# Branch A of a hybrid trunk layer: gate products between the projections, gates and scan handed out one piece per weight chunk

## The chip, the cores and the metric

The kernel runs on one core of a Trainium2 chip. The metric is the device time of one execution in microseconds. The median of three runs of the kernel before is 2580.13 us (2580.01 to 2581.76). The profile is one further execution of the same program.

## What is computed

One layer with 256 tokens, model width 4096 and two branches that read the same normalised input, then an output projection and a final norm. All inputs are float32.

```python
hn = rmsnorm(x, norm_g)
xa, ga, u, v, gb = split(hn @ w_in)                 # 5 x 4096 columns
xa = causal_depthwise_conv(xa, conv_w, conv_b)      # 4 taps
# branch A, 16 heads of 256 channels:
r = sigmoid(blockdiag(w_gate_a) xa + b_a)
i = sigmoid(blockdiag(w_gate_x) xa + b_x)
log_a = -8 * r * softplus(-lam)
h_t = exp(log_a_t) * h_(t-1) + sqrt(1 - exp(2 log_a_t)) * (i_t * xa_t)
ya = h * silu(ga)
# branch B, 16 head groups: yb = gelu(u) * (W_s layernorm(gelu(v)) + b) * silu(gb)
x = x + concat(ya, yb) @ w_out                      # 8192 x 4096
out = rmsnorm(x, final_g)
```

## The kernel before

Every float32 product is made of three float32r products: the operands are split into a high and a low part, and high times high, high times low and low times high are added in PSUM. The weights pass as one stream of chunks of 512 KB. For each chunk SyncE loads `raw` (four buffers), ScalarE rounds it into `hi`, VectorE subtracts to get `lo` (L64 to L66), and TensorE multiplies. `take` (L134) issues load and split of the chunk that is AHEAD = 3 further on; `hi` and `lo` have four buffers each, so the split of a chunk can begin when TensorE has left the chunk four before it. The order of chunks is the list `plan` (L69 to L86).

The elementwise work goes through a queue, `todo`: a finished product puts small functions there, and `work(n)` (L142), called after each chunk's products, takes n of them out and issues their instructions. `flush` issues all that is left. Within each engine, the framework's scheduler then sets the order of the built instructions by what it takes to be ready; the engines run their rows in that order.

Branch A (L533 to L566) takes two heads per round, in eight rounds. In a round TensorE runs four projections of 256 columns (`project`, L233; eight chunks of 16 products each), two for the heads' `xa` and two for their `ga`; then, after a `flush`, the gate products of both heads (`gate_products`, L473; 24 products a head, from one chunk of `w_g`); then the output projection of the round before (`out_project`, L286; 16 chunks of 12 products, and after every second chunk two additions `acc`, L284, on VectorE, which free two of the four PSUM buffers named `po`). `gate_values` (L487) reads the gate products on ScalarE: sigmoid twice, then tanh. A square root follows at L553; it needs another activation table than sigmoid and tanh, so an ACT_TABLE_LOAD stands ahead of it and another ahead of the next sigmoid. `queue_scan` (L499) has the rest of a head in seven steps: `one` for either channel half (add 1 and reciprocal on VectorE, L504 and L505), `two` and `three` (three products on GpSimd, L508, L509 and L513, and two instructions on VectorE), `four` (both scans, L518), `five` (GpSimd, L521) and `six` (the split of the result into `mix`). The steps of both heads are queued in pairs and handed out two per chunk in the output projection. The gate `ga` is collected at L271 to L273 (a copy on ScalarE, an addition on VectorE, a product on GpSimd) and made into a silu at L410 and L411.

In the last round the loads of `fg` (the final norm's gain, 2 MB on chip) and of eight further chunks of `w_out` that stay resident (`resident`, L530) go through the same SyncE queue. After it come eight chunks of the last products (L569) and sixteen slabs from the resident chunks (L579).

Of the kernel before, what the change touches and what calls it, by code (L numbers as in the profile page):

```python
# [7 lines left out]
F32 = mybir.dt.float32  # L8
# [18 lines left out]
def hybrid_trunk(ctx: ExitStack, tc: tile.TileContext, x, xt, par, w_p, w_t, w_g, ln_g, ln_b, ws_t, w_o, f_g, out):  # L27
    """Tokens are the moving or the stationary side of every product; a float32 product is three float32r
    passes over operands split exactly into 12 + 12 bits (high*high, high*low, low*high). The weights pass
    as one stream of chunks, split AHEAD chunks before their products; the elementwise work of a product is  # L30
    queued and handed out between the chunks that follow."""
# [23 lines left out]
    # a first use brings the activation tables in while the first loads run  # L55
# [27 lines left out]
    for e in range(8):  # L83
        plan += plan_p(X_A + 2 * e) + plan_p(X_A + 2 * e + 1) + plan_p(G_A + 2 * e) + plan_p(G_A + 2 * e + 1)
        plan += [("g", 2 * e, 0), ("g", 2 * e + 1, 0)] + plan_o(e - 1 if e else 15)
# [22 lines left out]
    def first_chunk(q):  # L108
        """The first chunks of x and of the weights, in step so that the products start early."""
# [24 lines left out]
    def take(*key):  # L134
        """The split chunk next in the plan; issues those up to AHEAD further on, and some queued work."""
        assert plan[issued[0] - len(ready)] == key, (plan[issued[0] - len(ready)], key)
        while issued[0] < len(plan) and len(ready) <= AHEAD:
            ready.append(load_chunk(plan[issued[0]]))
            issued[0] += 1
        return ready.pop(0)  # L140
# [5 lines left out]
    def flush():  # L146
        work(len(todo))

    def rsqrt_mean(dst, ssum, pool, n, name):
        """dst = 1 / sqrt(ssum / n + EPS), refined to float32."""  # L150
# [19 lines left out]
    # the tensor engine's clock rises under load: it is kept busy until the first chunks are there  # L170
# [27 lines left out]
    def queue_softplus():  # L198
        # 4 * softplus(-lambda): log1p(e^-|l|) = 2 atanh(z), z = s / (2 - s), s = sigmoid(-|l|)
# [33 lines left out]
    def project(block):  # L233
        """256 columns of the input projection, channels on partitions: [:, c, :256] + [:, c, 256:]."""
        ps = pj.tile([P, 2, 512], F32, tag="pj", name="ps")
        for q in range(KT // 4):
# [9 lines left out]
            work()  # L246
        return ps

    def project_t(slab):
        """512 columns of the input projection, tokens on partitions."""  # L250
# [17 lines left out]
    def collect(dst, ps, pool, tag):  # L268
        """dst = (the product in ps) * row scale."""
# [16 lines left out]
    def out_project(e, mix, extra=None):  # L286
        for n in range(8):
            ps = [po.tile([P, 512], F32, tag="po", name="po_t") for _ in range(2)]
            for q in range(2):
# [4 lines left out]
                work()  # L294
# [86 lines left out]
    def mix_tokens(i, ws, vn):  # L381
        """Position mixing of one head: chunk m of the tokens on partitions, [:, m, its 256 columns]."""
# [35 lines left out]
    for e in range(8):  # L418
# [16 lines left out]
        if pending is not None:  # L435
            out_project(*pending)
# [50 lines left out]
    def gate_values(h, both):  # L487
        gate = []
        for ps, bias, nm in zip(both, (B_A, B_X), "ri"):
            o = a2.tile([P, 2, S], F32, name=f"gate_{nm}")  # L490
            for c in range(2):
                nc.scalar.activation(o[:, c, :], ps[:, c, :], AF.Sigmoid, bias=prm_col(bias, 2 * h + c))
            gate.append(o)
        # t = tanh(-log a / 2): a = (1 - t) / (1 + t), sqrt(1 - a^2) = 2 sqrt(t) / (1 + t)
        for c in range(2):
            nc.scalar.activation(gate[0][:, c, :], gate[0][:, c, :], AF.Tanh, scale=sp4[:, 2 * h + c : 2 * h + c + 1])
        return gate

    def queue_scan(i, y, r, gi, g, mix):  # L499
        rec = a2.tile([P, 2, S], F32, name="rec")  # L500
        sq2 = a2.tile([P, 2, S], F32, name="sq2")
# [14 lines left out]
        def four():  # L516
            for c in range(2):
                nc.vector.tensor_tensor_scan(sq2[:, c, :], r[:, c, :], gi[:, c, :], 0.0, op0=ALU.mult, op1=ALU.add)  # L518
# [7 lines left out]
        return sq2, [lambda: one(0), lambda: one(1), two, three, four, five, six]  # L526
# [6 lines left out]
    for e in range(8):  # L533
        ys = []
# [6 lines left out]
        gs = []  # L541
        for i in range(2):
            g = a2.tile([P, 2, S], F32, name="ga")
            queue_silu(g, project(G_A + 2 * e + i), a3, "tmp")
            gs.append(g)
        flush()
        both = [gate_products(2 * e + i, *ys[i][1:]) for i in range(2)]
        mix = (mixp if e % 2 else mixa).tile([P, 4, 2, S], F32R, tag="mix", name="mix")
        gates = [gate_values(2 * e + i, both[i]) for i in range(2)]
        steps = []  # L550
        for i in range(2):
            sq2, st = queue_scan(i, ys[i][0], *gates[i], gs[i], mix)
            nc.scalar.activation(sq2, gates[i][0], AF.Sqrt, scale=4.0)  # L553
            steps.append(st)
        for pair in zip(*steps):
            todo.extend(pair)
# [7 lines left out]
        out_project(*pending, extra=None if e < 7 else lambda n: resident(n - 4) if n >= 4 else None)  # L564
        flush()
        pending = (e, mix)  # L566

# [87 lines left out]
```

## Time and profile before

| what | us |
|---|---|
| median of three runs | 2580.13 |
| span of the profiled execution | 2579.9 |
| TensorE busy in the span | 2542.5 (99%) |
| VectorE busy | 1599.4 (62%) |
| ScalarE busy | 1180.1 (46%) |
| GpSimd busy | 306.6 (12%) |

The profiled execution's own time, as far as the profile has it, is its span, 2579.9 us, which lies 0.2 us under the median of the runs. TensorE is the engine that sets the time; what matters of the others is where TensorE waits for them. Products overlap in TensorE's pipeline, so the starts of its rows are what tells its pace, and the profile's busy time does not show a slow restart as idle.

### The profile page before, as it was taken

Reading aid. Unit: us, or ns where it says so; the run is one execution under the profiler, and the core shown is the slowest. Engines: PE = TensorE matmul, PEld = TensorE weight load, DVE = VectorE, ACT = ScalarE, POOL = GpSimd, SP = SyncE. Lnnn points to the kernel's source line nnn. Section 1 sums busy time; section 2 is a strip of 40 time slices with the busy share of each in tenths; the row PEclk is TensorE's granted clock in tenths of the full one; section 3 lists DMA queues with packets and bytes.
Section 4 is the critical chain, followed back from the end, with each engine's and each line's share of the span. In section 5 each row is a group of like instructions: output and inputs, shape, how many; then the busy total and the mean of one; then the engine's idle time right before and its main releaser. Section 6 shows DMA issues by size and latency. Waiting matters only on the chain.

```text
span 2579.9 us, 32012 instructions
## 1 busy us (share of the span) xinstructions
PE 2542.5 (99%) x12306; PEld 2134.8 (83%) x12306; DVE 1599.4 (62%) x1731; ACT 1180.1 (46%) x1342; POOL 306.6 (12%) x234
## 2 busy tenths in 40 slices
PE   9999999999999999999999999999999999999997
PEld 7888888888888888888888888788888888788886
DVE  6544465564646565655555675858575766758586
ACT  7444444444444444444444534444453545344454
POOL 0000010110101010101000200202020201102034
PEclk9999999999999999999999999999999999999999
DMA  9655556565656565656555555555556565555564
GB/s 344 205 193 192 195 184 206 196 202 191 198 189 204 189 199 190 202 188 200 192 187 189 171 196 190 183 186 182 185 171 193 171 200 175 193 185 182 185 218 156
DMA packets 147849, 500.40 MB, mean 194 GB/s; under 512 B 16112, under 2 KB 26480, under 8 KB 147568
## 3 DMA queue, kind: packets, MB, share of 16 engines
q1 hardware_dynamic: 147552, 498.34, 58.8%
q8 instruction: 96, 1.57, 0.3%
q14 instruction: 57, 0.47, 0.1%
q10 hardware_dynamic: 144, 0.02, 0.0%
HBM read 494.10 MB, written 4.19 MB: 193 GB/s over the span
## 4 chain that ended last, share of the span: by engine, by line
PE 88%; DVE 8%; issue 3%; DMA 1%; ACT 1%; SPq 0%; DVEq 0%; ACTq 0%
PE ps L242 19%; PE ps L259 13%; PE ps L260 13%; PE ps L258 13%; PE ps L245 9%; PE po_t L278 6%; PE po_t L280 6%; PE po_t L279 6%; DVE lo L66 3%; DVE rec L504 1%; DVE sq L518 1%; DVE acc L284 1%; DVE rec L505 1%; DMA raw<-in_w_out 1%; ACT hi L65 1%
## 5 line engine op out<-in xcount | busy, mean ns | idle before, releaser
L66 DVE TENSOR_TENSOR lo<-raw,hi 128x1024 fp32r<-128x1024 f32 (+1 forms) x906 | 1135.8, 1257 | 893.2 <-ACT hi L65 892.7
L65 ACT CAST hi<-raw 128x1024 fp32r<-128x1024 f32 (+1 forms) x914 | 957.4, 1051 | 1281.1 <-PE ps L260 547.9
L242 PE MATMUL ps<-xs,hi 128*128 128x512 f32 x2048 | 722.3, 398 | 0.0
L259 PE MATMUL ps<-lo,xs 128*128 128x512 f32 x1536 | 598.0, 389 | 1.0 <-DVE lo L66 1.0
L258 PE MATMUL ps<-hi,xs 128*128 128x512 f32 x1536 | 598.8, 390 | 0.0
L260 PE MATMUL ps<-hi,xs 128*128 128x512 f32 x1536 | 597.6, 389 | 0.0
L245 PE MATMUL ps<-xs,lo 128*128 128x256 f32 x2048 | 574.9, 281 | 0.0
L242 PEld LDWEIGHTS ps<-xs,hi 128*128 128x128 f32 x2048 | 384.6, 188 | 94.4
L278 PE MATMUL po_t<-hi,mix 128*128 128x512 f32 x1026 | 400.6, 390 | 12.3 <-DVE acc L284 11.1
L279 PE MATMUL po_t<-lo,mix 128*128 128x512 f32 x1026 | 399.9, 390 | 10.3 <-DVE lo L66 10.3
L280 PE MATMUL po_t<-hi,mix 128*128 128x512 f32 x1026 | 399.2, 389 | 0.0
L245 PEld LDWEIGHTS ps<-xs,lo 128*128 128x128 f32 x2048 | 386.9, 189 | 0.3
L259 PEld LDWEIGHTS ps<-lo,xs 128*128 128x128 f32 x1536 | 288.6, 188 | 61.1 <-DVE lo L66 1.6
L258 PEld LDWEIGHTS ps<-hi,xs 128*128 128x128 f32 x1536 | 288.5, 188 | 60.3 <-ACT hi L65 0.7
L260 PEld LDWEIGHTS ps<-hi,xs 128*128 128x128 f32 x1536 | 288.5, 188 | 59.7
L278 PEld LDWEIGHTS po_t<-hi,mix 128*128 128x128 f32 x1026 | 192.6, 188 | 59.3 <-issue 15.7
L279 PEld LDWEIGHTS po_t<-lo,mix 128*128 128x128 f32 x1026 | 192.6, 188 | 52.7 <-DVE lo L66 13.7
L280 PEld LDWEIGHTS po_t<-hi,mix 128*128 128x128 f32 x1026 | 192.6, 188 | 39.9
L284 DVE TENSOR_TENSOR acc<-po_t,acc 128x512 f32<-128x512 f32 x256 | 164.4, 680 | 2.4 <-PE po_t L280 2.4
L340 POOL MEMSET ws<- 64x128 f32 x8 | 1.6, 201 | 723.2 <-DMA ws<-in_ws_t 386.5
L273 POOL TENSOR_TENSOR xp<-ev,rstd_bc 128x512 f32<-128x512 f32 x16 | 20.7, 1295 | 485.6 <-DVE ev L272 485.6
L358 POOL TENSOR_TENSOR v<-v,affine 128x256 f32<-128x256 f32 x32 | 38.7, 1227 | 286.1 <-DVE v L355 254.2
(124 smaller groups left out, 1073.3 us busy)
## 6 DMA issues: line engine op xcount, KB each, us to landing
raw<-in_w_t SPq DMA_DIRECT2D x382, 512.0 KB, 4.1
raw<-in_w_out SPq DMA_DIRECT2D x256, 512.0 KB, 3.3
raw<-in_w_p SPq DMA_DIRECT2D x256, 512.0 KB, 4.1
raw<-in_w_g SPq DMA_DIRECT2D x16, 512.0 KB, 3.3
acc<-in_x SPq DMA_DIRECT2D x8, 512.0 KB, 9.1
out<-acc SPq DMA_DIRECT2D x16, 256.0 KB, 2.8
xraw<-in_xt SPq DMA_DIRECT2D x14, 256.0 KB, 5.0
affine<-in_ln_g SPq DMA_DIRECT2D x16, 128.0 KB, 3.2
```

The source lines that it names most:

```text
L65: nc.scalar.copy(hi, src)
L66: sub.tensor_tensor(lo, src, hi.bitcast(F32), op=ALU.subtract)
L242: nc.tensor.matmul(ps[:, c, :], lhsT=hi[:, j, cs], rhs=xs[:, k, :, :].rearrange("p h t -> p (h t)"), start=k == 0, stop=False)
L245: nc.tensor.matmul(ps[:, c, 0:S], lhsT=lo[:, j, cs], rhs=xs[:, k, 0, :], start=False, stop=k == KT - 1)
L258: nc.tensor.matmul(ps[:, m, :], lhsT=xs[:, k, 0, ms], rhs=hi[:, j, :], start=k == 0, stop=False)
L259: nc.tensor.matmul(ps[:, m, :], lhsT=xs[:, k, 0, ms], rhs=lo[:, j, :], start=False, stop=False)
L260: nc.tensor.matmul(ps[:, m, :], lhsT=xs[:, k, 1, ms], rhs=hi[:, j, :], start=False, stop=k == KT - 1)
L278: nc.tensor.matmul(ps, lhsT=mix[:, k, 0, ms], rhs=hi[:, j, :], start=start, stop=False)
L279: nc.tensor.matmul(ps, lhsT=mix[:, k, 0, ms], rhs=lo[:, j, :], start=False, stop=False)
L280: nc.tensor.matmul(ps, lhsT=mix[:, k, 1, ms], rhs=hi[:, j, :], start=False, stop=stop)
L284: nc.vector.tensor_tensor(acc[:, m, ns], ps, acc[:, m, ns], op=ALU.add)
L358: nc.gpsimd.tensor_tensor(v[:, m, cs], v[:, m, cs], gain, op=ALU.mult)
```

## The change

In `plan` and in the round, the gate products of the first head move to between the second `xa` projection and the first `ga` projection, and those of the second head to between the two `ga` projections. The flush ahead of them is gone, except one in the last round, for the second gate's silu alone. `gate_values` becomes `queue_gates`: two sigmoids and then tanh with the square root are three queued pieces. `queue_scan` has eight pieces, with one scan each for the two channel halves. `project` and branch A's `out_project` hand out one piece per chunk; branch B and the last round keep two. The pieces of the first head's scan are queued when the second head's gate products have been issued.

```diff
-        plan += plan_p(X_A + 2 * e) + plan_p(X_A + 2 * e + 1) + plan_p(G_A + 2 * e) + plan_p(G_A + 2 * e + 1)
-        plan += [("g", 2 * e, 0), ("g", 2 * e + 1, 0)] + plan_o(e - 1 if e else 15)
+        plan += plan_p(X_A + 2 * e) + plan_p(X_A + 2 * e + 1) + [("g", 2 * e, 0)] + plan_p(G_A + 2 * e)
+        plan += [("g", 2 * e + 1, 0)] + plan_p(G_A + 2 * e + 1) + plan_o(e - 1 if e else 15)
...
-            work()
+            work(1)
         return ps
...
-    def out_project(e, mix, extra=None):
+    def out_project(e, mix, extra=None, items=1):
...
-                work()
+                work(items)
...
-    def gate_values(h, both):
+    def queue_gates(h, both):
+        r, gi = (a2.tile([P, 2, S], F32, name=f"gate_{nm}") for nm in "ri")
+        sq2 = a2.tile([P, 2, S], F32, name="sq2")
+        def sigmoid(o, ps, bias):
...
+        def decay():
+            for c in range(2):
+                nc.scalar.activation(r[:, c, :], r[:, c, :], AF.Tanh, scale=sp4[:, 2 * h + c : 2 * h + c + 1])
+            nc.scalar.activation(sq2, r, AF.Sqrt, scale=4.0)
+        todo.append(lambda: sigmoid(r, both[0], B_A))
+        todo.append(lambda: sigmoid(gi, both[1], B_X))
+        todo.append(decay)
+        return r, gi, sq2
...
-        return sq2, [lambda: one(0), lambda: one(1), two, three, four, five, six]
+        todo.extend([lambda: one(0), lambda: one(1), two, three, lambda: four(0), lambda: four(1), five, six])
...
-        gs = []
         for i in range(2):
+            gates = queue_gates(2 * e + i, gate_products(2 * e + i, *ys[i][1:]))
+            if i:
+                queue_scan(*scans.pop())
             g = a2.tile([P, 2, S], F32, name="ga")
-            queue_silu(g, project(G_A + 2 * e + i), a3, "tmp")
-            gs.append(g)
-        flush()
-        both = [gate_products(2 * e + i, *ys[i][1:]) for i in range(2)]
...
+            ps = project(G_A + 2 * e + i)
+            scans.append((i, ys[i][0], *gates, g, mix))
+            if e == 7 and i:
+                rest, todo[:] = todo[:], []
+                queue_silu(g, ps, a3, "tmp")
+                flush()
+                todo.extend(rest)
+            else:
+                queue_silu(g, ps, a3, "tmp")
+        queue_scan(*scans.pop())
```

VectorE, first round of branch A, the kernel before: from the copy of the second `ga` product (`ev`) on, that is from the gate products to the third pair of output chunks. `lo` is a chunk's split, `acc` the additions that free PSUM.

```order
L272 TENSOR_TENSOR ev<-ps,ev 128x512
L504 TENSOR_SCALAR rec<-gate_r 128x256
L505 RECIPROCAL rec<-rec 128x256
L66 TENSOR_TENSOR lo<-raw,hi 128x1024
L504 TENSOR_SCALAR rec<-gate_r 128x256
L505 RECIPROCAL rec<-rec 128x256
L504 TENSOR_SCALAR rec<-gate_r 128x256 x2
L505 RECIPROCAL rec<-rec 128x256 x2
L66 TENSOR_TENSOR lo<-raw,hi 128x1024 x2
L284 TENSOR_TENSOR acc<-po_t,acc 128x512 x2
```

Both heads' four reciprocals stand here in one run of rows, ahead of two splits and the first additions; this run leaves the place.

The same engine with the change, in the second `ga` projection: from the copy of the first `ga` product on. The splits named here are those of this projection's chunks 3 to 7 and of the first output chunks; `mix` is the first head's.

```order
L272 TENSOR_TENSOR ev<-ps,ev 128x512
L66 TENSOR_TENSOR lo<-raw,hi 128x1024 x2
L511 TENSOR_SCALAR rec<-gate_r 128x256
L66 TENSOR_TENSOR mix<-ga,mix 128x2x256
L512 RECIPROCAL rec<-rec 128x256
L511 TENSOR_SCALAR rec<-gate_r 128x256
L512 RECIPROCAL rec<-rec 128x256
L66 TENSOR_TENSOR lo<-raw,hi 128x1024 x2
L517 TENSOR_SCALAR gate_r<-gate_r 128x512
L66 TENSOR_TENSOR lo<-raw,hi 128x1024
L521 TENSOR_TENSOR gate_r<-gate_r,rec 128x512
```

The second head's reciprocals have come into the projection, behind the split of the first head's `mix` and ahead of the splits of chunks 5 and 6; the first head's have gone into the projection before it.

SyncE, last round, the kernel before: the loads from the two gate chunks (`in_w_g`) to the end; `in_w_out` are output chunks, the resident ones among them.

```order
L98 DMA raw<-in_w_g 128x1024 x2
L98 DMA raw<-in_w_out 128x1024 x6
L563 DMA fg<-in_f_g 128x4096
L98 DMA raw<-in_w_out 128x1024 x26
L610 DMA out<-acc 128x512 x16
```

The load of `fg` stands behind the sixth output chunk here. With the change, from that round's second gate chunk on (`in_w_p` are chunks of the projections):

```order
L98 DMA raw<-in_w_g 128x1024
L98 DMA raw<-in_w_p 128x1024 x8
L98 DMA raw<-in_w_out 128x1024 x9
L571 DMA fg<-in_f_g 128x4096
L98 DMA raw<-in_w_out 128x1024 x23
```

The load of `fg` has moved three output chunks back in the queue, and the gate chunk ahead of a projection.

## Rows read from the trace of the kernel before

**Rows 1.** Page, part 1: busy us of each engine (share), instructions.
```profile
PE 2542.5 (99%) x12306; PEld 2134.8 (83%) x12306; DVE 1599.4 (62%) x1731; ACT 1180.1 (46%) x1342; POOL 306.6 (12%) x234
```

**Rows 2.** Stretches: from:to length, busy by engine, PEclk, DMA share, GB/s.
```profile
1376.30:2519.00 1142.70, 1123.16 (x6019) 959.80 (x6017) 778.45 (x848) 528.62 (x612) 183.48 (x131) 1.00 0.57 186
...
1376.30:1465.13 88.83, 88.83 (x515) 78.33 (x513) 49.61 (x56) 37.43 (x40) 5.77 (x8) 1.00 0.58 190
...
1470.89:1518.20 47.31, 44.86 (x197) 36.24 (x196) 43.76 (x49) 22.56 (x29) 14.65 (x9) 1.00 0.54 178
```

**Rows 3.** Who TensorE waited for in branch A: us, times, longest.
```profile
PE po_t L279 <- DVE lo L66: 10.3, 8, 1.3
PE po_t L278 <- DVE acc L284: 8.2, 8, 1.0
```

**Rows 4.** Timeline of TensorE, first output projection: start, us, what, idle before.
```profile
1479.07 0.39 PE L278 MATMUL po_t<-hi,mix 128*128 128x512 f32 x1
1480.76 0.50 PE L279 MATMUL po_t<-lo,mix 128*128 128x512 f32 x1 [1.30 <-DVE lo L66]
1481.09 0.40 PE L280 MATMUL po_t<-hi,mix 128*128 128x512 f32 x1
...
1483.15 0.39 PE L280 MATMUL po_t<-hi,mix 128*128 128x512 f32 x1
1483.66 0.47 PE L278 MATMUL po_t<-hi,mix 128*128 128x512 f32 x1
...
1494.44 0.39 PE L280 MATMUL po_t<-hi,mix 128*128 128x512 f32 x1
1495.85 0.47 PE L278 MATMUL po_t<-hi,mix 128*128 128x512 f32 x1 [1.02 <-DVE acc L284]
```

**Rows 5.** Timeline of VectorE in the same stretch.
```profile
1471.12 1.38 DVE L504 TENSOR_SCALAR rec<-gate_r 128x256 f32<-128x256 f32 x1
...
1476.27 3.35 DVE L505 RECIPROCAL rec<-rec 128x256 f32<-128x256 f32 x2
1479.55 3.37 DVE L66 TENSOR_TENSOR lo<-raw,hi 128x1024 fp32r<-128x1024 f32 x2
...
1490.51 3.48 DVE L518 TENSOR_TENSOR_SCAN sq<-gate_r,gate_i 128x256 f32<-128x256 f32 x4
```

**Rows 6.** Timelines of ScalarE and GpSimd in the same stretch.
```profile
1469.55 0.63 ACT L410 ACTIVATE sg<-ga 128x512 f32<-128x512 f32 x1 [0.20 <-POOL ga L273]
...
1473.18 1.28 ACT L553 ACT_TABLE_LOAD   x1
1474.47 1.15 ACT L553 ACTIVATE sq<-gate_r 128x512 f32<-128x512 f32 x2
...
1493.47 0.62 ACT L65 CAST mix<-ga 128x512 fp32r<-128x512 f32 x1 [2.82 <-POOL ga L521]
...
1468.20 1.31 POOL L273 TENSOR_TENSOR ga<-ev,rstd_bc 128x512 f32<-128x512 f32 x1 [18.62 <-DVE ev L272]
1470.25 2.10 POOL L411 TENSOR_TENSOR ga<-ga,sg 128x512 f32<-128x512 f32 x1 [0.74 <-ACT sg L410]
...
1491.85 1.59 POOL L521 TENSOR_TENSOR ga<-ga,sq 128x512 f32<-128x512 f32 x1 [7.79 <-DVE sq L518]
```

**Rows 7.** One line and one group: durations (ns min/median/max); busy us, mean ns, idle before.
```profile
L504 DVE TENSOR_SCALAR rec<-gate_r x32: 284/1113/1393, 1468.0 to 2476.3; 128x256 f32<-128x256 f32 x32
...
L66 DVE TENSOR_TENSOR lo<-raw,hi 128x1024 fp32r<-128x1024 f32 (+1 forms) x906 | 1135.8, 1257 | 893.2 <-ACT hi L65 892.7
```

**Rows 8.** The second round's four projections as one stretch.
```profile
1517.73:1608.17 90.44, 90.44 (x513) 78.38 (x512) 49.41 (x55) 38.13 (x39) 5.41 (x6) 1.00 0.57 186
```

**Rows 9.** The end: chain of waits; TensorE's waits after 2519 us; DMA issue, KB, us to landing.
```profile
2498.84 3.46 DMA raw<-in_w_out
...
PE po_t L278 <- DVE acc L284: 2.9, 3, 2.0
...
fg<-in_f_g SPq DMA_DIRECT2D x1, 2048.0 KB, 7.5
```

More of the change, by code (lines that the diff above doesn't have):

```diff
@@ L435, in hybrid_trunk @@
         if pending is not None:
-            out_project(*pending)
+            out_project(*pending, items=2)
         mix = mixp.tile([P, 4, 2, S], F32R, tag="mix", name="mix")
@@ L485, in gate_products, with queue_scan @@
         return both
-    def gate_values(h, both):
-        gate = []
-        for ps, bias, nm in zip(both, (B_A, B_X), "ri"):
-            o = a2.tile([P, 2, S], F32, name=f"gate_{nm}")
+    def queue_gates(h, both):
+        r, gi = (a2.tile([P, 2, S], F32, name=f"gate_{nm}") for nm in "ri")
+        sq2 = a2.tile([P, 2, S], F32, name="sq2")
+        def sigmoid(o, ps, bias):
             for c in range(2):
                 nc.scalar.activation(o[:, c, :], ps[:, c, :], AF.Sigmoid, bias=prm_col(bias, 2 * h + c))
[L493 to L499, printed above, removed]
+        def decay():
[6 more added lines that the diff above has]
+        return r, gi, sq2
+    def queue_scan(i, y, r, gi, sq2, g, mix):
         rec = a2.tile([P, 2, S], F32, name="rec")
-        sq2 = a2.tile([P, 2, S], F32, name="sq2")
         def one(c):
@@ L514, in three, with four @@
             nc.vector.tensor_tensor(r, r, rec, op=ALU.mult)
-        def four():
-            for c in range(2):
-                nc.vector.tensor_tensor_scan(sq2[:, c, :], r[:, c, :], gi[:, c, :], 0.0, op0=ALU.mult, op1=ALU.add)
+        def four(c):
+            nc.vector.tensor_tensor_scan(sq2[:, c, :], r[:, c, :], gi[:, c, :], 0.0, op0=ALU.mult, op1=ALU.add)
         def five():
@@ L533, in hybrid_trunk @@
     for e in range(8):
+        mix = (mixp if e % 2 else mixa).tile([P, 4, 2, S], F32R, tag="mix", name="mix")
         ys = []
@@ L540, in hybrid_trunk @@
             ys.append((y, yh, yl))
-        gs = []
+        scans = []
         for i in range(2):
+            gates = queue_gates(2 * e + i, gate_products(2 * e + i, *ys[i][1:]))
+            if i:
+                queue_scan(*scans.pop())
             g = a2.tile([P, 2, S], F32, name="ga")
-            queue_silu(g, project(G_A + 2 * e + i), a3, "tmp")
-            gs.append(g)
-        flush()
-        both = [gate_products(2 * e + i, *ys[i][1:]) for i in range(2)]
[L548 to L556, printed above, removed]
+            ps = project(G_A + 2 * e + i)
[8 more added lines that the diff above has]
+        queue_scan(*scans.pop())
         if e == 7:
@@ L563, in hybrid_trunk @@
             nc.sync.dma_start(fg, f_g.partition_broadcast(P))
-        out_project(*pending, extra=None if e < 7 else lambda n: resident(n - 4) if n >= 4 else None)
-        flush()
+        out_project(*pending, extra=None if e < 7 else lambda n: resident(n - 4) if n >= 4 else None, items=1 if e < 7 else 2)
         pending = (e, mix)
+    flush()
     for n in range(8):
```

## The prediction, made before the changed kernel was run

> **What bounds the kernel now.** I began with the page's busy times: TensorE works 99% of the span and no other engine more than 62% [rows 1]. So a change gains only where TensorE stands still, and costs only where it makes TensorE wait. The stretches tell how much there is: in branch A's eight rounds TensorE is busy 1123.16 of 1142.70 us [rows 2], so 19.5 us are idle. The waits name the places: in each of the eight rounds one wait for a split `lo` (10.3 us in all) and one for an addition `acc` (8.2) [rows 3]; 18.5 of the 19.5 us. The reader is to see that the count is eight, one of each per round, and that all lie in the output projection: the four projections and the gate products have none (88.83 busy of 88.83 in the first round's projections [rows 2]).
>
> The idle column is not all that such a wait costs, so I went to TensorE's timeline and took starts [rows 4]. From 1481.09 to 1483.15 nine steps take 2.06 us, 0.23 each. The product at 1480.76 starts 1.69 us after the one before it, 1.46 too late; the next follows after 0.33 instead of 0.23, 0.10 more for a slow restart; at 1483.66 0.51 have passed, 0.28 too many; at 1495.85 1.41, 1.18 too many; behind each of the last two I count another 0.08 of restart, by the 0.10 above. Together 3.18 us a round, **25.4 us in eight rounds**. This is the pool that the change can empty.
>
> Why VectorE is late is in its own timeline [rows 5]. After the gate products the reciprocals of both heads run together; one pair takes 3.35 us, and only behind it come two splits (3.37). The split that TensorE waits for at 1480.76 is the first of them. Later four scans in one run take 3.48 us, and the addition that frees PSUM at 1495.85 is behind them. A chunk of the output projection lasts 12 x 0.23 = 2.7 us, and VectorE was busy 43.76 of 47.31 us in that stretch [rows 2]: it is nearly full there, and a run of 3.4 us is not absorbed. In the projections it was busy 49.61 of 88.83 us [rows 2]; there is the room.
>
> **The change part by part.** TensorE's instructions are the same in number and kind; the gate chunks only stand elsewhere in the stream. Nothing is saved on any engine. VectorE's four reciprocals, the two `rec` additions and the scans move from the output projection into the two `ga` projections, one head in each. By the built order VectorE's output-projection rows keep only splits, additions, one copy addition and one `mix` split. From 43.76 us I take four reciprocals (2 x 3.35 = 6.7), the scans (3.48) and one split of `mix` (half of what they were), and it falls to about 33 of 44 us: both waits of [rows 3] should go. **Term 1: -25.4 us**, if nothing new comes.
>
> What is new: the second `ga` projection carries the second head's gates and the first head's silu, product and `mix`. Its order on VectorE: splits of chunks 3 and 4, one `rec` addition, the split of `mix`, reciprocal, `rec` addition, reciprocal, split of chunk 5. VectorE waits for `mix` there, with the splits of chunks 5, 6 and 7 queued behind the wait, and TensorE waiting for those. I count from the start of chunk 0 of that projection. In the trace the product with `rstd` on GpSimd began at 1468.20, 3.1 us after its projection ended at 1465.13 [rows 2, 6]; the second gate products (24 x 0.12 = 2.9 us, half of the 5.76 from 1465.13 to 1470.89, [rows 2]) now lie between, so it begins at +0.2. From its start to the end of the silu product took 4.15 us (1468.20 to 1470.25 + 2.10), then the product with the scan 1.59 and ScalarE's rounding of `mix` 0.62 [rows 6]: `mix` is there at +6.6. Then VectorE: two `rec` additions, two reciprocals 3.35, the `mix` split 0.68 (half a chunk's 1.26 and a little over, from [rows 7]), the split of chunk 5 1.26. With the additions at their least, 0.28 each, that is 5.85 us, ready at +12.4. With both at their worst, 1.39 each [rows 7], and the split of chunk 5 delayed by one GpSimd product of 1.31 [rows 6], it is +15.9. TensorE needs it at 5 x 90.44/32 = +14.1 [rows 8]. So the cover is 1.7 us at best and short by 1.8 at worst. I take a value near the good end, because one of the two additions waits for nothing on GpSimd: its next product there needs the very reciprocal that follows. One blocked addition gives +13.5, 0.6 to spare. Chunks 6 and 7 follow with less behind them. **Term 2: +1.2 us**, 0.15 a round; bounds 0 and 8 x 2.0 = 16 us.
>
> The long row of 1.38 against 0.28 for the same addition is VectorE standing while GpSimd runs: the row at 1471.12 ends with GpSimd's product, 1470.25 + 2.10 [rows 5, 6]. The Trainium skill ("SBUF — State Buffer", section "Who interferes with whom") states that the two engines share one port pair, that whoever starts first holds it for its whole instruction and the other blocks fully, and that a VectorE instruction with two SBUF inputs is among those that block. By that rule this change does harm: it puts six GpSimd products beside the splits of one projection. The trace agrees; with the rule in force at every step the sum is the bad bound of term 2, without it the good one.
>
> ScalarE loads its activation table four times a round instead of twice: 16 more of 1.28 us [rows 6], 20.5 us on an engine that was busy 37.43 of 88.83 us in the projections [rows 2]. Two of them lie in the second `ga` projection and the next rounding is not due before VectorE gets to it, so I count zero; that cover is the 5.85 us of VectorE work above, and without it a load costs its 1.28 a round.
>
> The gate chunks' loads are single ones among projection chunks now. No load row is added; SyncE's queue passes them in the same order as TensorE uses them. Count zero.
>
> The pace of TensorE in the projections is the open size. The first round's four took 88.83 us, the second's 90.44 [rows 2, 8], for the same products, with no wait in either: 1.61 us more. The first round is entered from the end of branch B, the others straight from output products. Now the two `ga` projections of a round are entered from gate products, which no row shows. Bounds: all seven later rounds gain half of 1.61 (-5.6 us); or the first round loses its half (+0.8). I take 0, since gate products pass into a projection without a break, as the output products do in those later rounds. **Term 3: 0**, bounds -5.6 and +0.8.
>
> The end: after 2519 us TensorE waits three times for additions, 2.9 us, with restarts some 3.3 [rows 4, 9]. The chain there goes through loads of `w_out` from 2498.84 on [rows 9], which waited for `raw` buffers that late splits (behind scans and `mix`) held. With those splits in time the loads start earlier. Against it, the 2 MB of `fg` (7.5 us to landing [rows 9]) stand three chunks later, closer to the resident loads. Bounds: all 3.3 gained, or 3 lost. **Term 4: -2.2 us**, two thirds, since `fg` lands before the eight resident loads begin.
>
> Sum: 2579.9 - 25.4 + 1.2 + 0 - 2.2 = 2553.5 for the profiled execution; the median lies 0.2 above its span: **2553.7 us**.
>
> **The rivals.** (a) VectorE late in the second `ga` projection: the bad bound above, 0.5 to 1.8 us a round with restart, 4 to 16 us: 2556.5 to 2568. For it: VectorE and GpSimd do collide in rows. Against: collisions at every step are needed. (b) The pace: the `ga` projections run at the first round's pace, 2548. (c) The end keeps or adds to its waits: 2556 to 2559. (d) Table loads delay ScalarE. The sum has a load at 1.28 us, and in the trace the square root starts 0.01 us after the load ends [rows 6]. If each load cost twice that, the silu's sigmoid and the tanh would come 1.28 later, which eats the 0.6 to spare and leaves it 0.7 short, with a restart 0.8 a round: 6.4 us instead of term 2's 1.2, 2559. The Trainium skill ("ScalarE: Activation LUTs", section "What ACT_TABLE_LOAD costs") states a drain of about 1.38 us behind each load, and its rules ask to do all of one set before switching, which this change breaks; the trace does not show that drain. (e) The waits only move: each round's 3.2 us come back as waits for splits in the `ga` projections. No change, 2580; it needs the bad bound of term 2 and 1.4 us more in each round. (f) **Slower**: the wait for `mix` on VectorE. Should the first head's scan slip out of its own projection by a chunk (2.8 us), and the GpSimd products ahead of `mix` that ran at 1.31 and 1.59 take 2.1 as the third did, `mix` comes at +6.6 + 2.8 + 1.3 = +10.7 and the split of chunk 5 at +16.5 to +20.0, 2.4 to 5.9 us late. With a restart each that is 20 to 48 us lost in eight rounds against the 27.4 (terms 1 and 4) gained: up to 2600. It decides from 3.4 us late on.
>
> **How the numbers follow.** My forecast (all or nearly all waits gone, 2551 to 2556) 0.50; (a) 0.20; (b) 0.13; (c) 0.06; (d) 0.04; (e) 0.04; (f) 0.03. The range runs from (b), with the end's 3.3 gained too, to most of (a): 2546 to 2565. A measurement of this kernel tells 0.2%, 5 us, from no change: faster is all but (e) and (f), 0.93; same 0.04; slower 0.03.
>
> **What would show it.** Right: no wait of `po_t` for `lo` or `acc` in rounds 1 to 7, and a round of 143.0 us, gate product to gate product (1465.13 to 1608.17 [rows 2, 8]), down to about 139.9. Term 2 shows as a wait of `ps` (L245's product) for `lo` in the second `ga` projection. Term 3 shows in the length of eight chunks behind a gate product: 22.2 or 22.6 us. Term 4 shows in the three waits after the last round. Wrong: waits of over 0.6 us a round for `lo` in the `ga` projections, or a VectorE row of `mix` that starts later than 7 us into the second of them.

## The result, and the profile after

The changed kernel takes 2552.38 us (median of four runs, 2550.41 to 2553.06) against 2580.07 before; the ratio is 0.989, with a 95% interval of 0.9876 to 0.9904. It is faster by 1.1%, and 2553.7 had been predicted. The profiled execution took 2552.63 us for a span of 2550.8, so 1.8 us lie outside the span. The page of the kernel after, part 1, against [rows 1]:

```profile
PE 2530.9 (99%) x12306; PEld 2137.6 (84%) x12306; DVE 1625.9 (64%) x1731; ACT 1203.3 (47%) x1360; POOL 322.0 (13%) x234
```

TensorE has the same 12306 products. VectorE is busy 26.5 us longer with the same 1731 instructions. The largest part are the sixteen rows of L517 (L510 before), which take 1.52 instead of 0.42 us each, 17.6 us in all; in the second round such a row runs from 1601.97 on, beside a GpSimd product that lasts from 1601.04 to 1603.20. ScalarE has 18 more instructions and 23.2 us more, which is 18 table loads of 1.28. All TensorE's waits of the kernel after, against [rows 3] (line and tile that waited, for whom; us, times, longest):

```profile
PE po_t L278 <- DVE acc L284: 3.7, 1, 3.7
PE warm L173 <- POOL ones L169: 1.1, 1, 1.1
PE ps L259 <- DVE lo L66: 0.9, 2, 0.7
```

Of the sixteen waits in the eight rounds none is left. The two last lines belong to the kernel's start; the first is new and lies at the end, behind the product of 2488.62. Stretches of the second round of the kernel after (length, busy by engine, PEclk, DMA share, GB/s): its two `xa` projections, its two `ga` projections, its output projection, and last all of the round.

```profile
1513.74:1536.34 22.60, 22.60 (x130) 19.61 (x128) 10.79 (x10) 8.40 (x8) 0.00 (x0) 1.00 0.59 190
1536.34:1558.95 22.61, 22.61 (x131) 19.62 (x129) 13.84 (x18) 9.50 (x10) 1.40 (x2) 1.00 0.58 187
1561.83:1584.02 22.19, 22.19 (x131) 19.56 (x129) 21.99 (x26) 11.88 (x14) 7.32 (x5) 1.00 0.48 157
1586.90:1609.09 22.19, 22.19 (x130) 19.56 (x129) 19.16 (x18) 13.55 (x19) 10.72 (x6) 1.00 0.49 162
1609.09:1652.65 43.56, 43.56 (x194) 36.04 (x193) 30.73 (x34) 19.64 (x20) 4.75 (x3) 1.00 0.67 214
...
1513.74:1652.65 138.91, 138.91 (x753) 120.15 (x752) 99.94 (x107) 68.54 (x78) 24.19 (x16) 1.00 0.59 190
```

The reader is to see three things. VectorE's load has moved: 30.73 of 43.56 us in the output projection, 21.99 and 19.16 of 22.19 in the `ga` projections; these are now the fullest places. The two projections behind gate products take 22.19 us, the two behind other products 22.60. And the clock is at its upper level throughout (1.00, 2.4 GHz). The last round with all that follows it, to the end of the span, of before and of after (each from a window of its own):

```profile
2376.05:2579.90 203.85, 185.56 (x951) 156.01 (x949) 138.10 (x170) 94.98 (x131) 57.97 (x34) 0.98 0.56 186
```

```profile
2347.22:2550.80 203.58, 185.60 (x951) 158.25 (x949) 145.75 (x170) 98.55 (x134) 59.30 (x34) 0.96 0.56 187
```

So the gain by stages, from TensorE's starts:

| stage | before | after | difference | predicted |
|---|---|---|---|---|
| to the first round | 1376.30 | 1375.57 | -0.7 | 0 |
| first round | 141.43 | 138.17 | -3.3 | -3.0 |
| next six rounds | 858.32 | 833.48 | -24.8 | -18.2 |
| last round and end | 203.85 | 203.58 | -0.3 | -5.2 |
| span | 2579.9 | 2550.8 | -29.1 | -26.4 |

The rounds gained more than was predicted and the end gained nothing. The end, in TensorE's timeline of the kernel after (start, us, what, idle before):

```profile
2488.62 0.39 PE L280 MATMUL po_t<-hi,mix 128*128 128x512 f32 x1
2492.74 0.76 PE L278 MATMUL po_t<-hi,mix 128*128 128x512 f32 x1 [3.73 <-DVE acc L284]
2493.30 0.63 PE L279 MATMUL po_t<-lo,mix 128*128 128x512 f32 x1
```

and the granted clock there, in stretches:

```profile
2492.70:2498.50 5.80, 5.76 (x14) 4.54 (x15) 5.80 (x5) 1.54 (x3) 2.38 (x1) 0.51 0.62 200
2498.50:2510.00 11.50, 11.50 (x52) 9.51 (x51) 10.81 (x14) 6.05 (x6) 6.17 (x3) 1.00 0.64 208
```

One stall of 4.12 us from start to start, 3.89 too many. Behind it the granted clock is 0.51, the lower level of 1.2 GHz, for 5.8 us: fourteen products, nearly all 0.43 instead of 0.23 us from start to start, 2.7 us more. Together 6.6 us are lost there, against 3.8 in the kernel before (7.0 from 2440 on by the same count, less the 3.2 of its last round). Behind TensorE's last product the rest of the span is 1.4 us longer too (14.5 against 13.1): VectorE's scaling of the first token half, in a row of 1.77 us beside GpSimd's products, stands ahead of the last additions. In the kernel before such a row (1.78 us, from 2563.67 on) came ahead of the last products, and TensorE waited 0.2 us there. VectorE's timeline of the kernel after, where the last product starts at 2536.27:

```profile
2535.67 1.77 DVE L613 SCALAR_TENSOR_TENSOR acc<-acc,rs,fg 128x512 f32<-128x512 f32 x1
2537.36 0.68 DVE L599 TENSOR_TENSOR acc<-po_t,acc 128x512 f32<-128x512 f32 x1
2537.96 0.74 DVE L613 SCALAR_TENSOR_TENSOR acc<-acc,rs,fg 128x512 f32<-128x512 f32 x1
2538.62 1.34 DVE L599 TENSOR_TENSOR acc<-po_t,acc 128x512 f32<-128x512 f32 x3
```

### The profile page after: what moved, and what is told of

It is laid out like the page before. It is cut to its first block, busy times and chain, and to the rows that moved or that the text cites. A ratio compares the mean times of both kernels' runs of the same rounds, so it can differ in the third digit from the quotient of the medians.

```text
span 2550.8 us, 32030 instructions
## 1 busy us (share of the span) xinstructions
PE 2530.9 (99%) x12306; PEld 2137.6 (84%) x12306; DVE 1625.9 (64%) x1731; ACT 1203.3 (47%) x1360; POOL 322.0 (13%) x234
## 4 chain that ended last, share of the span: by engine, by line
PE 97%; DMA 1%; DVE 1%; ACT 0%; POOL 0%; issue 0%; SPq 0%; DVEq 0%; ACTq 0%
PE ps L242 19%; PE ps L259 14%; PE ps L260 14%; PE ps L258 14%; PE ps L245 10%; PE po_t L278 8%; PE po_t L280 8%; PE po_t L279 8%; DMA raw<-in_w_out 1%; PE pgate L482 1%; PE pgate L483 1%; PE pgate L481 1%; ACT hi L65 0%; POOL lo L66 0%; PE pt L404 0%
```

## Experiments

**Which half of the change brings the gain.** One kernel has the moved gate products, but no handing out by single pieces: the gates are issued at once, both scans of a head are one piece again, and two pieces are taken per chunk everywhere:

```diff
-            work(1)
+            work()
...
-        todo.append(lambda: sigmoid(r, both[0], B_A))
-        todo.append(lambda: sigmoid(gi, both[1], B_X))
-        todo.append(decay)
+        sigmoid(r, both[0], B_A)
+        sigmoid(gi, both[1], B_X)
+        decay()
...
-        todo.extend([lambda: one(0), lambda: one(1), two, three, lambda: four(0), lambda: four(1), five, six])
+        todo.extend([lambda: one(0), lambda: one(1), two, three, four, five, six])
...
```

> Half of the change: the gate products stand between the projections, but sigmoid, tanh and square root are issued at once, both scans of a head are one piece, and two pieces are handed out per chunk everywhere. Theory (what counts is that the reciprocals run beside projections, where VectorE has room): no TensorE waits in the rounds, within 2 us of the changed kernel, 2550 to 2554. Rival (the handing out is what counts): runs of reciprocals hold the splits in the ga projections, 1 to 3 us a round, 2560 to 2575.

It took 2560.83 us (ratio 0.9924, 0.9909 to 0.9939), span 2560.3. Its waits:

```profile
PE ps L245 <- DVE lo L66: 6.3, 8, 0.8
PE po_t L278 <- DVE acc L284: 3.7, 1, 3.7
```

The output projections are clean, but one wait a round for a split stands in the second `ga` projection, which takes 23.25 to 23.45 us instead of 22.19. That is rival (a)'s wait, at rival (a)'s place, and the rival of this experiment was right, not its theory. The other kernel leaves the gate products where they were and hands out single pieces, with the scans halved (`work(1)` in `project`, `items=1` in branch A's `out_project`, `four` in two pieces). It also queues the first head's pieces ahead of the second's, instead of in pairs, and drops the flush at a round's end, as the changed kernel does:

> The other half: the kernel before with the gate products where they were, the scans halved, one piece handed out per chunk and no flush at a round's end. Theory (VectorE's work in the output projection is the limit there, 43.8 of 47.3 us, however it is cut): waits for lo and acc stay, 1 to 3 us a round, projections at 90.4 us; 2568 to 2580. Rival (only the runs of four reciprocals and four scans hold TensorE up): the waits go, 2579.9 - 25.4 = 2554.5 or a little less.

It took 2584.06 us (ratio 1.0013, 1.0004 to 1.0023), span 2581.7:

```profile
PE po_t L279 <- DVE lo L66: 17.4, 10, 2.2
PE po_t L278 <- DVE acc L284: 4.5, 4, 1.8
```

Each of the first seven rounds has one wait for a split, of 2.2 us, in place of two shorter ones. In four of them the granted clock falls to 0.5 behind it, and those output projections take 47.6 to 47.7 us; in the three others they take 46.1, against 46.8 to 46.9 before. So the move is worth 19.6 us of span (2579.9 to 2560.3; 19.9 by the medians). The handing out does not pay by itself, 3.4 us more by the medians, of which the falls of the clock are a part, and it gives 9.5 us on top of the move (8.5 by the medians): the eight waits in the second `ga` projections go with it.

**How near the wait for `mix` is.** Rival (f) named the point from which the change would be slower than no change. One or two idle GpSimd products ahead of the first head's product with its scan bring `mix` later:

```diff
         def five():
+            for _ in range(2 if i == 0 else 0):
+                nc.gpsimd.tensor_tensor(gi, g, sq2, op=ALU.mult)
             nc.gpsimd.tensor_tensor(g, g, sq2, op=ALU.mult)
```

> Two extra GpSimd products (about 1.3 us each, results overwritten by nothing that is read; outputs unchanged) ahead of the first head's product with its scan, so that its mix comes about 2.6 us later in the second ga projection of each round. It doubles the disputed wait: the cover that I read there is 1.0 to 1.2 us. Theory: TensorE waits for the split of chunk 5 in rounds 1 to 7, 1.4 to 1.6 us each and 0.1 for the restart, 10 to 13 us in all; span 2561 to 2564. Rival: VectorE has its cover elsewhere (the rows behind the wait reorder their durations because fewer of them collide with GpSimd): waits under 0.4 us a round, span 2551 to 2554.

It took 2578.32 us (one run), span 2576.5: nearly all the gain was gone. VectorE's row of `mix` and the split behind it, and TensorE's product that waits for that split, in the second round:

```profile
1600.14 0.69 DVE L66 TENSOR_TENSOR mix<-ga,mix 128x512 fp32r<-128x512 f32 x1 [3.09 <-ACT mix L65]
...
1604.35 3.38 DVE L66 TENSOR_TENSOR lo<-raw,hi 128x1024 fp32r<-128x1024 f32 x2
```

```profile
1603.28 0.39 PE L242 MATMUL ps<-xs,hi 128*128 128x512 f32 x1
1605.57 0.39 PE L245 MATMUL ps<-xs,lo 128*128 128x256 f32 x1 [1.90 <-DVE lo L66]
...
1606.18 0.63 PE L242 MATMUL ps<-xs,hi 128*128 128x512 f32 x1
```

The projection began at 1589.40, so `mix` came 10.74 us into it instead of 7.56, 3.18 later; the product came 2.05 us late (2.29 from the one before it instead of 0.23). The difference, 1.13 us, is the cover that was read from the timeline. What was not expected is the price behind it: in the steps after the wait the granted clock is 0.56 in this round. In the fourth round the same wait is followed by the upper level:

```profile
1605.60:1609.40 3.80, 3.80 (x14) 3.27 (x15) 3.80 (x3) 0.24 (x1) 3.19 (x2) 0.56 0.61 180
...
1890.90:1894.70 3.80, 3.79 (x22) 3.33 (x23) 3.80 (x3) 0.68 (x2) 3.24 (x2) 1.00 0.58 169
```

With the lower clock that chunk takes 6.52 instead of 2.77 us, 3.7 lost for a wait of 2.0. The clock fell in five of the eight rounds, whose second `ga` projections are 3.7 to 3.8 us longer than 22.19; in the other three they are 2.2 to 2.3 longer. The profile counts eight waits of 15.2 us together, but the span grew by 25.7.

> One extra GpSimd product instead of two ahead of the first head's product with its scan; outputs unchanged. With two, mix came 3.18 us later (10.74 instead of 7.56 us into the second ga projection) and chunk 5's first lo product 2.05 us late, so the cover is 1.1 us. One product should bring mix some 1.4 to 1.6 us later: a wait of 0.3 to 0.5 us a round, 3 to 5 us with the restarts, no half clock behind it, span 2554 to 2556. If the half clock follows such a short wait too, some 8 us more, 2562 to 2564.

With one product instead of two the span was 2552.2 (2554.02 us, one run), below what was expected. VectorE had been held to 7.56 us by a stretched addition anyway, so its row of `mix` came only 0.6 us later; with that row itself at 1.17 us, the split of chunk 5 came 1.1 us later, which is all the cover. The second `ga` projections took 22.28 to 22.40 us instead of 22.19, and the clock stayed.

**The end.** First the load of `fg`:

```diff
-            nc.sync.dma_start(fg, f_g.partition_broadcast(P))
...
+        if n == 6:
+            nc.gpsimd.tensor_copy(fg[:, 0:1], acc[:, 1, n * 512 : n * 512 + 1])
+            nc.sync.dma_start(fg, f_g.partition_broadcast(P))
```

> The changed kernel with one thing moved: the 2 MB load of fg waits for an addition of the seventh of the last eight chunks (a one-column copy on GpSimd makes it wait), so it stands behind all loads of w_out. Theory (the load of fg, three chunks later than before, drains the raw buffers just as the resident loads begin): the wait of 3.9 us after the last round and the 2.7 us at half clock behind it go; span 2550.8 - 6.6 = 2544, up to 2546 if GpSimd's products with fg then come late; TensorE's granted clock stays at 1.00 there. Rival (the eight resident loads alone, three chunks per 5.4 us, outrun the buffers): the wait stays, 2550 to 2552.

It took 2551.14 us (0.9871 to 0.99), span 2549.3, as its rival had it; its runs (2550.38 to 2551.27) lie within those of the changed kernel. The stall is cut in two, 2.75 and 1.61 us too many, and no lower clock follows. The place of this load therefore shapes the stall but doesn't make it: 4.5 us remain with the restarts. What else is there are the splits of the resident chunks, which GpSimd subtracts. In the kernel after, one of them (POOL) and VectorE's split beside it, which takes 1.21 alone:

```profile
2481.70 2.41 POOL L66 TENSOR_TENSOR lo<-raw,hi 128x1024 fp32r<-128x1024 f32 x1 [4.54 <-ACT hi L65]
```

```profile
2482.61 2.59 DVE L66 TENSOR_TENSOR lo<-raw,hi 128x1024 fp32r<-128x1024 f32 x1 [2.03 <-ACT hi L65]
...
2486.32 1.21 DVE L66 TENSOR_TENSOR lo<-raw,hi 128x1024 fp32r<-128x1024 f32 x1
```

The next experiment gives these subtractions to VectorE:

```diff
-        res.append(load_split(("o", 15, n), resp, resp, f"r{n}", sub=nc.gpsimd))
+        res.append(load_split(("o", 15, n), resp, resp, f"r{n}"))
```

> The low part of the eight resident chunks is subtracted on VectorE instead of GpSimd; all else is as in the changed kernel. My theory of the end: GpSimd's split of a resident chunk (2.4 us) blocks VectorE's split beside it (3.4 us for two becomes 2.5 us for one), so raw buffers come free late, the loads of the last output chunks fall behind, and TensorE stands 3.9 us and then runs at half the clock for fourteen steps (6.6 us lost together). Without those GpSimd rows the stall shrinks below 1 us or goes, no half clock follows, and the span comes to 2544 to 2547 us (2550.8 in the changed kernel). Rival 1, the loads themselves set the pace of three chunks in about 6.9 us whoever subtracts: stall of 3 to 4 us again, span 2549 to 2552. Rival 2, VectorE is too full with eight more splits: longer waits for lo or acc in the last round, span 2552 to 2556.

It took 2549.03 us (ratio 0.9876, 0.986 to 0.9893), span 2547.1, 3.7 less than the changed kernel's (3.4 by the medians). VectorE's timeline, two splits in less than the one took, and TensorE's at the stall:

```profile
2480.34 2.36 DVE L66 TENSOR_TENSOR lo<-raw,hi 128x1024 fp32r<-128x1024 f32 x2 [0.93 <-ACT hi L65]
```

```profile
2490.25 0.47 PE L278 MATMUL po_t<-hi,mix 128*128 128x512 f32 x1 [1.18 <-ACT hi L65]
```

Three short stalls are left, 1.34, 0.26 and 0.53 us too many, and the clock stays at 1.00. The stalls of 6.6 us have come down to 2.4 with the restarts; 2.7 of the difference is the lower clock, which is gone. Of the four executions of the changed kernel one had a mean granted clock of 0.998 instead of 0.996 and a span of 2548.6, so the lower clock does not seem to come in every one, and against that span this kernel's four (2546.4 to 2547.6) gain only 1.0 to 2.2 us.

The stall did not shrink below 1 us as the theory had it, and the chain of waits of the kernel after shows another path than the theory. Of VectorE's stretched splits only the last (2489.46, 2.53 us) stands in it, right ahead of the addition that TensorE waits for. Up to there it runs through GpSimd's own split, in a ring that repeats every 6.8 to 7.0 us:

```profile
2474.75 2.42 POOL lo L66
...
2477.19 3.36 DMA raw<-in_w_out
...
2480.58 1.06 ACT hi L65
...
2481.70 2.42 POOL lo L66
```

A load starts when GpSimd's split of a resident chunk has ended; behind it come ScalarE's rounding and GpSimd's next split. With VectorE doing the split (1.2 us in the ring instead of 2.4) the loads in that kernel's chain take 4.0 to 4.4 us instead of 3.3, so only about 0.5 us a turn is gained; what is left of the stall is a wait for a rounding, behind a load. To that extent the rival that the loads set the pace is right.

**The pace of the projections.** Three kernels put extra products of 256 columns ahead of the first projection of rounds 1 to 7 (1, 2 or 24 of them), as gate products stand ahead of the fast ones:

```diff
+            for j in range(lead if q == 0 else 0):
+                nc.tensor.matmul(ps[:, 0, 0:S], lhsT=hi[:, j % 4, 0:P], rhs=xs[:, j % 4, 0, :], start=True, stop=True)
```

> The changed kernel with one extra product of 256 columns ahead of the first projection of rounds 1 to 7 (its sum is overwritten by the first real product). Theory (a projection's pace is set by what TensorE ran just ahead of it: behind 256-column gate products it is 2.773 us a chunk, behind 512-column output products 2.827): the two xa projections go from 45.2 to 44.4 us in each of seven rounds, 7 x 16 x 0.054 = 6.0 us less, 0.8 us for the extra products; span 2545.6. Rival (the pace follows from something else, the gate run's length or its buffers): 2551.6, 0.8 us more than without.

> Two extra products instead of twenty-four, at the same place. They cost 7 x 2 x 0.12 = 1.7 us. If the number of steps ahead decides (an odd step shifts which product of a group of three meets a slow step), one extra product, which left the xa projections at 2.827 us a chunk, and two may differ: xa projections at 2.773 and a span of about 2546.5. If a long run or something else with the gate products decides, xa stays at 2.827 and the span is about 2552.5. I hold the second more likely, 3 to 1.

> Twenty-four extra products of 256 columns (into a PSUM tile that the first real product then overwrites; the outputs don't change) stand ahead of the first projection of rounds 1 to 7, as gate products stand ahead of the two fast projections. They cost 7 x 24 x 0.12 = 20.2 us. Theory A: a run of such products, with nothing else behind it, is what sets the pace of the sixteen-product chunks that follow; then the two xa projections of these rounds go from 2.827 to 2.773 us a chunk, 7 x 16 x 0.054 = 6.0 us come back and the span is about 2565. Theory B: the pace is set by something that comes with the gate products' place (their weight chunk, the PSUM tile, the stream of loads): xa projections stay at 2.827, span about 2571.

They took 2555.5 (median of four; span 2555.5 in the profile), 2556.46 (one run, span 2554.7) and 2576.07 us (one run, span 2574.3), all more than the extra products explain. With two of them, the first `xa` and both `ga` projections of the second round:

```profile
1514.60:1537.21 22.61, 22.61 (x130) 19.60 (x129) 10.56 (x10) 8.39 (x8) 0.00 (x0) 1.00 0.58 186
1562.71:1585.32 22.61, 22.61 (x130) 19.60 (x129) 22.01 (x26) 11.79 (x15) 7.30 (x5) 1.00 0.50 164
1588.20:1610.39 22.19, 22.19 (x131) 19.56 (x129) 19.16 (x18) 13.59 (x19) 10.73 (x6) 1.00 0.48 157
```

Not only did the `xa` projections stay slow; the first `ga` projection, which stands behind real gate products, turned slow too. The same in all three. So short products ahead do not set the pace by themselves, and what happened two projections earlier still counts. Then the order within the projections was changed, on top of the version with the resident splits on VectorE: in each half chunk four products with `hi` and then four with `lo`, instead of pairs.

> On top of the version with the resident split on VectorE: in branch A's projections the products of each half chunk stand as four with hi, then four with lo, instead of in pairs; the products are the same. Disputed: what makes the projections behind the output products slower than those behind gate products (22.60 against 22.19 us for 128 products). Theory A, the order of long and short steps sets the pace: with four and four every projection takes the same time, near or under 22.19, whatever stands ahead of it; the xa projections of seven rounds give back up to 14 x 0.41 = 5.8 us, span 2541 to 2543 (2547.1 before this edit). Theory B, something else that comes with the place (weights' loads, PSUM) slows them: the xa projections stay at 22.6, span 2546 to 2548. Slower is possible: in a run of four short steps each takes 0.120, as in the gate products, instead of 0.113 to 0.117, at worst 0.02 us per four, 16 a projection: +0.3 us each, 8 to 10 us in all.

It took 2550.97 us, span 2549.0. Every projection takes 22.43 to 22.52 us, whatever stands ahead of it. With fours the place makes 0.09 us at most, with pairs 0.4, so the order of the steps bears on the pace. The expectation was wrong in the size: 22.45, not 22.19, so the `ga` projections lost more than the `xa` projections gained. Turning round only the first eight products of a round,

> On top of the version with the resident split on VectorE: only the first eight products of rounds 1 to 7 are turned round, four with hi and then four with lo; all else stays in pairs. If the pace of a projection is taken on at its start and kept, this may switch the two xa projections to 22.19 us: span 2541 to 2542. If it depends on each step's own surroundings, they stay at 22.60 and the span at 2547. An extra run of short steps at the entry did not switch them in three kernels, so I hold the second more likely, 2 to 1.

left the `xa` projections at 22.58 and 22.61 us (one run, span 2547.2). Last, fours in the `xa` projections of rounds 1 to 7 and pairs in the `ga` projections, with the resident splits on VectorE:

> On top of the version with the resident split on VectorE: four products with hi and then four with lo in the xa projections of rounds 1 to 7 alone, where pairs take 22.60 and fours took 22.43 to 22.45 us; the ga projections keep pairs, which take 22.19 there. If the ga projections keep that pace: 7 x (0.17 + 0.16) = 2.3 us less, span 2544 to 2546 (2547.1 without). If a projection's pace is taken on from what stands ahead of the gate products, one or both ga projections of a round may fall to 22.60: up to 14 x 0.42 = 5.9 us more, span 2548 to 2551. I hold the first more likely, 3 to 2, since gate products switched the pace at this place in every kernel without extra products.

It took 2546.08 us (2545.44 to 2546.59; ratio 0.9865, 0.9849 to 0.9882), span 2544.8, the fastest of all. The first `xa` and the first `ga` projection of the second round:

```profile
1513.59:1536.02 22.43, 22.43 (x130) 19.62 (x128) 10.79 (x10) 8.69 (x9) 0.00 (x0) 1.00 0.57 188
1561.35:1583.54 22.19, 22.19 (x131) 19.56 (x130) 21.99 (x25) 11.87 (x14) 6.26 (x5) 1.00 0.45 154
```

Why pairs have two paces, and why an extra product two projections earlier turns the first `ga` projection slow, stays open.

## Why the prediction was right, and where it was not

**Term 1 (-25.4) held in the rounds.** All sixteen waits are gone, and the kernel with the moved order alone shows that the move emptied the output projections. The 3.18 us a round came in full: the first round, whose pace did not change, gained 3.26. From gate product to gate product a later round took 138.9 us, where 139.9 was named; most of the difference is term 3.

**Term 2 (+1.2) was zero.** The working was sound step by step; by its own chosen value 0.6 us were to spare, so the 1.2 was an allowance. In the second round of the kernel after, GpSimd's product with `rstd` started and ScalarE's rounding of `mix` ran at

```profile
1587.09 1.32 POOL L273 TENSOR_TENSOR ga<-ev,rstd_bc 128x512 f32<-128x512 f32 x1 [9.88 <-DVE ev L272]
```

```profile
1592.19 0.62 ACT L65 CAST mix<-ga 128x512 fp32r<-128x512 f32 x1 [0.29 <-POOL ga L527]
1592.83 1.28 ACT L500 ACT_TABLE_LOAD   x1
1594.12 0.64 ACT L500 ACTIVATE sq<-gate_r 128x512 f32<-128x512 f32 x1
```

that is +0.2 (predicted +0.2) and ready at +5.9 (predicted +6.6) into the projection that starts at 1586.90. VectorE's rows from there:

```profile
1593.16 1.38 DVE L511 TENSOR_SCALAR rec<-gate_r 128x256 f32<-128x256 f32 x1
1594.46 0.68 DVE L66 TENSOR_TENSOR mix<-ga,mix 128x512 fp32r<-128x512 f32 x1
1595.06 1.74 DVE L512 RECIPROCAL rec<-rec 128x256 f32<-128x256 f32 x1
1596.72 0.22 DVE L511 TENSOR_SCALAR rec<-gate_r 128x256 f32<-128x256 f32 x1
1596.98 1.75 DVE L512 RECIPROCAL rec<-rec 128x256 f32<-128x256 f32 x1
1598.65 3.39 DVE L66 TENSOR_TENSOR lo<-raw,hi 128x1024 fp32r<-128x1024 f32 x2
```

One addition of 1.38 and one of 0.22, as the chosen value had it. The row of `mix` starts at +7.56, behind the long addition; a start later than 7 us had been named as a sign of being wrong, and it came true without any wait, so that sign was set too early. The split of chunk 5 starts at +11.75 and with 1.2 us is ready at +13.0, against a need at +14.1. The cover is 1.1 us where 0.6 was counted, so no wait comes. The experiment with two more GpSimd products measured the same 1.13. The Trainium skill ("SBUF — State Buffer", "Who interferes with whom") states for VectorE's two-port modes that whichever of VectorE and GpSimd issues first gets the shared ports for its whole instruction and the other blocks. The trace agrees with the blocking, and no row shows the mode: the addition that met GpSimd's product took 1.38, the one that met none 0.22. The harm stayed inside the cover. Rival (a)'s bad bound needed the collision at every step up to the split of chunk 5; of these it happened at one.

**Term 3 (0) was wrong: -5.9, 0.3 past its low bound of -5.6.** The step that failed is the reason given for taking 0, that gate products pass into a projection without a break as output products do. Both `ga` projections of the seven later rounds take 22.19 us, as in the first round, where before they took 22.61: 14 x 0.42 = 5.9 us. That is what rival (b) said, at its full size. The bound was nearly right, and no row of the kernel before has a projection behind gate products, which could have told the two ends apart. The runs with extra products show that such a pace can't be argued from the neighbour's kind; what sets it stays open.

**Term 4 (-2.2) had the wrong sign.** The failed step is that the waits of the end came from late splits behind scans and `mix`. Those splits are in time now, and the stalls grew from 3.8 to 6.6 us. The phase with resident chunks is short of time by itself: it asks for three chunks in two output chunks (5.44 us), and in the kernel after the ring of GpSimd's split, load and rounding lets the resident splits begin every 6.8 to 7.0 us (2467.93, 2474.75, 2481.70, 2488.55); with VectorE doing them the pairs of splits began every 6.4 on average (2467.98 to 2487.14). What that phase lacks is about the same in the kernel before (3.8 us), in the kernel after (3.9 without the clock) and with `fg` last (4.5); it falls to 2.4 when the resident splits leave GpSimd. In the kernel after it comes in one piece, and the lower clock's 2.7 us come on top. By the table, with -3.2 of term 1 and -0.8 of the pace in the last round, term 4 is +3.8 (rounded): 2.8 in the stalls, 1.4 behind the last product, and 0.5 the other way, part of it the wait of 0.2 in the last products of the kernel before. Rival (c) had the effect, with +3 at most.

**The sum.** Terms 2, 3 and 4 missed by -1.2, -5.9 and +6.0, the start by -0.7 (with the same instructions up to there, the traces of the experiments have 1375.25 to 1376.20), and the rounds' small rest by -0.9; they nearly cancel, which is why 2553.5 stands beside a span of 2550.8. The profiled execution's own time was also mis-sized: 0.2 us were taken for what lies outside the span, and it is 1.8. (The span 2579.9 fits the highest of the three runs before, 2581.76, not the median.) The forecast was right in its mechanism, and closer in its number than its terms deserved.

**The rivals.** (d) A table load costs its 1.28 us and no more: it starts at 1592.83, 0.02 us after the row ahead of it, and the square root starts 0.01 us after its end, at 1594.12. The Trainium skill ("ScalarE: Activation LUTs", "What ACT_TABLE_LOAD costs") states a drain of about 1.38 us with each load, which no row here shows. (e) Waits that only move came with the order alone, 6.3 of 18.5 us, not with the whole change. (f) The slower case was not reached: with the split 2.05 us late in each of the eight rounds, 25.7 of the 29.1 us of span that had been gained were lost. In proportion the change would be slower from about 2.3 us late on (an estimate from these two numbers), not from 3.4: the working of (f) took the loss as the wait with a restart, and the lower clock behind five of the eight waits came on top.

## What to carry to other kernels

Work moved out of a full stage should be counted against the cover of the first consumer in the new stage, instruction by instruction; that count was right to half a microsecond here, and a deliberate delay of the suspected input measures the cover directly. Moving the producer made the gain, and handing its work out in single pieces only paid once it had been moved. An engine that takes over work (GpSimd's splits here) can stand in the ring that brings the next load. A gain that repeats per round need not hold for the last round: there the next phase's own rate decides, and a single stall can cost more than its idle time.

## What the hardware showed that was not expected

- The same 128 products took 22.60 or 22.19 us at a granted clock of 1.00, with no wait in either, and fours instead of pairs 22.43 to 22.52 wherever they stood.
- The lower clock (0.51 and 0.56 in the stretches shown) followed an idle time of 3.73 us at the end and of 1.90 us in five rounds of the delayed kernel. The same 1.90 us was followed by 1.00 in its three other rounds, and the idle time of 2.59 us with `fg` last by normal steps:

```profile
2492.14 0.47 PE L278 MATMUL po_t<-hi,mix 128*128 128x512 f32 x1 [2.59 <-DVE acc L284]
2492.44 0.40 PE L279 MATMUL po_t<-lo,mix 128*128 128x512 f32 x1
```

So the length of one stall alone does not tell whether the clock falls.
